# An expert-overflow loop moved ahead of the last expert pair, and the last down projection, its sum and the final norm taken by column halves

## Chip, cores and metric

The kernel runs on one core of a Trainium2 chip. The metric is the device time of one launch in microseconds (us). The kernel before has a median of 1254.08 us over 3 runs (1251.48 to 1255.8).

## The reference

Two transformer blocks run in a row on 256 tokens of width 1024. The change touches only the end of the second: a mixture of 32 experts of which every token uses two, a residual, and a last RMS norm.

```python
def hier_moe(h, w_rg, b_rg, w_re, b_re, w_gate, w_up, w_down):
    ...
    top_val, top_idx = lax.top_k(in_grp, MOE_TOP_K)
    gate = grp_p[:, None] * jax.nn.softmax(top_val, axis=-1)
    ...
    def run_block(args):
        xb, e = args
        hid = jax.nn.silu(xb @ w_gate[e]) * (xb @ w_up[e])
        return hid @ w_down[e]
    ...
    out = jnp.zeros((T + 1, D), jnp.float32).at[slot_tok].add(
        ys.astype(jnp.float32) * slot_gate[:, None])[:T]

def second_block(x, c, ada_w, ada_b, norm_mix_g, norm_ffn_g, final_g,
    ...
        h = rmsnorm_2(x, norm_ffn_g[i]) * (1 + sc2) + sh2
        x = x + g2 * hier_moe(h, moe_w_rg[i], moe_b_rg[i], moe_w_re[i], moe_b_re[i],
                              moe_w_gate[i], moe_w_up[i], moe_w_down[i])
    return rmsnorm_2(x, final_g)
```

## The kernel before

All weights are f32 and are read once. Every expert has 6 MB: gate, up and down matrices of 2 MB, each in two blocks of 1 MB. Experts go in 16 pairs (`for i in range(NP)`, L1752), and a pair needs 12 tiles of 1 MB; `moe_w` holds tiles 0 to 191 in that order, so the last pair is tiles 180 to 191. Tile q goes into slot q mod 21 of a ring made of five pools (names in the trace: ew, nw, raw, wr, hl). `preload(n)` (L1115) issues loads on SP until n tiles are issued; `weights(b)` of pair i calls it with 12 i + 2 b + 21. SP gives its loads the semaphores DMAHW0 to DMAHW7 in turn and waits for the old one before it issues a new one.

Each expert has 64 token slots in these pairs, whose token rows (`xg`) are gathered ahead. `expert` (L1614) does for a pair the blocks b = 0 to 3: b = 0 and 1 gate, b = 2 and 3 up, each of 8 matmuls, four per expert; the two experts fill the two halves of the 128 output rows. Then the SiLU (ACT) and the product `hid` (DVE). `down` (L1636) first calls `back(0)` and `back(1)`, which hold the previous pair's way back to the tokens (`combine2`, sums in four PSUM banks `acc`) and this pair's `way_back` (transposes of the one-hot matrix, L1603), then does blocks b = 4 and 5 of the down matrix into two banks `py` of the tag "w", which has two buffers.

In the last pair (`final`), `spread(0)` (L1713) puts the row g2 on all partitions between gate and up; `back` calls `gather_up` (L1723) for both token halves: R = acc * g2 + X, eight DVE operations, and after that `way_back` copies its result (L1611). At `back(5)` four matmuls with a zero (`zo`, L1773) open the `acc` banks again. After `down`, DVE multiplies both halves of `py` by g2 into `y` (L1659).

An expert with over 64 tokens needs more blocks of 64. Their number is in `nblk`, computed on the chip. After the last pair each engine loads it (L1786), and a loop `tc.For_i(0, n_more, 1)` (L1787) does one block per turn, loading 6 tiles by itself. Then the tail: four f32 matmuls (`combine`, L1671) bring `y` back to the tokens, DVE adds them to R, ACT squares and sums (L67), POOL raises to -1/2 (L253), `spread(1)` puts the norm's gain on all partitions, DVE scales (L79), and SP issues four output DMAs (L1835).

The engines' order is the program's order; nothing is reordered between engines except by waits.

Of the kernel before, what the change touches and what calls it, by code (L numbers as in the profile page):

```python
# [18 lines left out]
D = 1024  # L19
# [21 lines left out]
def kernel(ctx, tc, A, out, stop=None):  # L41
# [1556 lines left out]

    def way_back(oh_g, n, exact=False, into=None):
# [35 lines left out]

    def down(hid, weights, n_e, y, before=lambda j: None, scaled=False, gates_of=None):  # L1636
        n = 64 * n_e
# [6 lines left out]
        before(1)  # L1644
        py = [pbank("w"), pbank("w")]
        for b in range(4, 6):
            ws = weights(b)
            before(b)
            for kk in range(2):
                k = 2 * (b - 4) + kk  # L1650
                for c in range(2):
                    for e in range(n_e):
                        T.matmul(py[c][64 * e:64 * e + 64, :], hT[:, k, 64 * e:64 * e + 64],  # L1653
                                 ws[e][:, kk * 1024 + c * 512:kk * 1024 + (c + 1) * 512],
                                 start=k == 0, stop=k == 3)
        if scaled:
            for c in range(2):
                sl = slice(512 * c, 512 * c + 512)
                tt(y[:n, sl], py[c][:n], end[0][:n, sl], MUL)  # L1659
        else:  # L1660
            gc = gates_of()
            for c in range(2):
                sl = slice(512 * c, 512 * c + 512)
                act(yh[:, sl], py[c], AF.Copy, scale=gc)
                stt(yl[:, sl], py[c], gc, yh[:, sl].bitcast(F32), MUL, SUB)

# [5 lines left out]

    def combine2(h, og_, first, last):

        for c in range(2):
            sl = slice(512 * c, 512 * c + 512)
# [23 lines left out]

    zo = moe.tile([1, 2], BF16, name="zo")
    G.memset(zo[:, 0:1], 0.0)
    G.memset(zo[:, 1:2], 1.0)
    end = []

    def start_ends():
# [3 lines left out]
        G.dma_start(rows_[0:1, D:2 * D], A["final_g"])  # L1710
        end.extend([rows_[:, 0:D], rows_[:, D:2 * D], R, ring.tile([128, 2048], F32, name="raw", tag="raw")[:, 0:D]])

# [27 lines left out]
    def start():  # L1740
# [9 lines left out]
        V.tensor_copy(nblk, upto[0:1, 31:32])  # L1750

    for i in range(NP):  # L1752
# [5 lines left out]
        final = i == NP - 1  # L1758

        def back(j, i=i, prev=prev, final=final):  # L1760
# [6 lines left out]
            if j == 1:  # L1767
                backs[i] = way_back(onehots[i], 128, not final)
# [9 lines left out]
        hid = expert(weights, 2, (lambda: spread(0)) if final else None, None if i else start, 128 * (i % 2))  # L1778
        down(hid, weights, 2, end[3] if final else None, back, scaled=final, gates_of=lambda i=i: backs[i][1])
        prev = backs[i]  # L1780


    bt = rtile("bt", 1, pool=moe)
    V.memset(bt, 0.0)
    spare = nexts.tile([128, 2048], F32, name="nw", tag="nw")
    n_more = nc.values_load(nblk[0:1, 0:1], min_val=0, max_val=7)  # L1786
    with tc.For_i(0, n_more, 1):  # L1787
        oe = spare[:, D + 256:D + 288]
        ts(oe, upto, bt, None, ALU.is_gt)
        stt(oe, before, bt, oe, ALU.is_le, MUL)  # L1790
        tmp = moe.tile([128, 32], F32, name="more", tag="more")
        sel = moe.tile([128, 8], F32, name="sel")

        def pick(j, src):
            tt(tmp, src, oe, MUL)
            red(sel[:, j:j + 1], tmp, ADD)
        for h in range(2):
            pick(h, rank[:, h, :])
            pick(2 + h, gate[:, h, :])
        pick(4, before)  # L1800
        pick(5, iota64[:, 0:32])
        tt(sel[:, 6:7], bt, sel[:, 4:5], SUB)
        ts(sel[:, 6:7], sel[:, 6:7], 1.0, 64.0, ADD, MUL)
        ts(sel[0:1, 5:6], sel[0:1, 5:6], FAR, None, ADD)
        eid = moe.tile([1, 1], I32, name="eid")
        V.tensor_copy(eid, sel[0:1, 5:6])
        e_reg = nc.values_load(eid[0:1, 0:1], engines=(mybir.EngineType.SP,), min_val=0, max_val=NEXP - 1)
        oh_r = spare[:, D + 288:D + 544].rearrange("p (h t) -> p h t", h=2)
        oh_g = moe.tile([128, 2, 128], F32, name="oh", tag="oh_g", bufs=1)
        for h in range(2):  # L1810
            tt(sel[:, h:h + 1], sel[:, h:h + 1], sel[:, 6:7], SUB)
            for t_, sc in ((oh_r, rstd[h][:, 0:1]), (oh_g, sel[:, 2 + h:3 + h])):
                ts(t_[:, h, 0:64], iota64, sel[:, h:h + 1], sc, EQ, MUL)
        gather(oh_r, 64)
        og_ = way_back(oh_g, 64, into=spare[:, D:D + 256].rearrange("p (h t) -> p h t", h=2))

        def weights(b):
            t_ = wring.tile([128, 2048], F32, name="wr", tag="wr")
            SP.dma_start(t_, A["moe"][bass.ds(e_reg, 1), b].rearrange("a p n -> p (a n)"))
            return [t_]  # L1820
        hid = expert(weights, 1)
        y2 = spare[:, 0:D]
        down(hid, weights, 1, y2, scaled=True)
        for h in range(2):
            combine(h, og_, y2, False, False, 64)
        ts(bt, bt, 1.0, None, ADD)
    last = {}
    R, frow = end[2], end[1]

    def finish(h):  # L1830
        for c in range(2):
            sl = slice(512 * c, 512 * c + 512)
            o = R[:, h, sl]
            stt(o, R[:, h, sl], last[h], frow[:, sl], MUL, MUL)
            SP.dma_start(out[0, h * 128:(h + 1) * 128, sl], o)  # L1835

    for h in range(2):
        ss = stats.tile([128, 2], F32, name="fs", tag=f"fs{h}", bufs=1)
        for c in range(2):
            sl = slice(512 * c, 512 * c + 512)  # L1840
            combine(h, prev, end[3], False, True, cs=(c,))
            tt(R[:, h, sl], R[:, h, sl], acc[h, c], ADD)
            act(hid, R[:, h, sl], AF.Square, scale=D ** -0.5, accum_out=ss[:, c:c + 1])
        ts(ss[:, 0:1], ss[:, 0:1], EPS, ss[:, 1:2], ADD, ADD, e=G)
# [3 lines left out]
    for h in range(2):  # L1848
        finish(h)

# [174 lines left out]
```

## Time and profile before

| | us |
|---|---|
| median of 3 runs (lowest, highest) | 1254.08 (1251.48, 1255.8) |
| the profiled execution's own time | 1258.29 |
| its span in the trace | 1256.5 |
| PE, DVE, ACT busy in the span | 1191.1, 655.1, 481.4 |

A page of the profile shows one execution. Its span starts with the first and ends with the last record. Rows of the timeline give start, duration, engine, line, operation, tiles and count; equal neighbours are merged into one row (x32), and brackets tell how long the engine stood idle before and what ended that. An f32 matmul of the program leaves two records. Weight loads have rows of their own (PEld). An engine name with a q (SPq, ACTq) is that engine's sequencer: register loads, branches and waits. No row of the trace comes from lines 1788 to 1826, the loop's body.

### The profile page before, as it was taken

The numbers are of one execution on the slowest core, as the hardware profiler recorded it, in microseconds if no ns is written. First come the engines' busy times: TensorE is split into PE (matmuls) and PEld (weight loads), VectorE is DVE, ScalarE is ACT, GpSimd is POOL, SyncE is SP. The second block draws the span as 40 slices with busy tenths as digits, with TensorE's granted clock in tenths as the row PEclk, the third lists the DMA queues.
The fourth block names the chain that finished last, engine by engine and source line by source line (L and its number), as shares of the span: only waits on it lengthen the run. The fifth ranks groups of instructions, "written<-read, shape, count | busy, mean of one in ns | idle before, by whom it ended". The sixth has DMA issues, their size and how long they took to land. (4 is left out here: it accounts for less than half of the span.)

```text
span 1256.5 us, 15660 instructions
## 1 busy us (share of the span) xinstructions
PE 1191.1 (95%) x6064; PEld 816.7 (65%) x6067; DVE 655.1 (52%) x1112; ACT 481.4 (38%) x800; POOL 76.0 (6%) x105
## 2 busy tenths in 40 slices
PE   7999999999889999999998979999999999898996
PEld 5888888888777788888887947444444444343432
DVE  6767777677767687765464985422112221111114
ACT  7546544446775474444364523311101111010111
POOL 1101000001030000000003240000000000000000
PEclk9999999999999999999998989999999999999998
DMA  9644787774533189765543768699999999999992
GB/s 333 234 171 184 262 288 264 282 301 145 188 142 113 46 329 374 282 239 196 201 162 146 262 210 326 260 421 420 419 420 420 419 420 420 420 420 421 420 419 97
DMA packets 59947, 361.14 MB, mean 287 GB/s; under 512 B 7200, under 2 KB 10432, under 8 KB 21600
## 3 DMA queue, kind: packets, MB, share of 16 engines
q1 hardware_dynamic: 58752, 357.21, 73.2%
q0 software_dynamic: 976, 2.92, 0.7%
q8 instruction: 48, 0.79, 0.2%
q14 instruction: 27, 0.22, 0.1%
q10 hardware_dynamic: 144, 0.00, 0.0%
HBM read 358.15 MB, written 1.96 MB: 287 GB/s over the span
## 5 line engine op out<-in xcount | busy, mean ns | idle before, releaser
L111 PE MATMUL mm<-hl,xTh 128*128 128x512 f32 (+3 forms) x1376 | 422.1, 386 | 11.7 <-ACT hl L66 6.2
L70 DVE TENSOR_TENSOR hl<-raw,hl 128x1024 fp32r<-128x1024 f32 (+3 forms) x240 | 283.6, 1212 | 88.5 <-ACT hl L66 84.8
L111 PEld LDWEIGHTS mm<-hl,xTh 128*128 128x128 f32 x1376 | 257.0, 191 | 61.8 <-ACT hl L66 6.6
L66 ACT ACTIVATE hl<-raw 128x1024 fp32r<-128x1024 f32 (+3 forms) x240 | 240.7, 1033 | 137.3 <-PE mm L111 108.6
L111 PE MATMUL mm<-hl,xTl 128*128 128x512 f32 (+3 forms) x688 | 266.1, 387 | 2.5 <-DVE xTl L70 2.5
L111 PEld LDWEIGHTS mm<-hl,xTl 128*128 128x128 f32 x688 | 131.4, 191 | 26.0 <-DVE xTl L70 3.2
L70 DVE TENSOR_TENSOR hid<-gu,hid 128x512 f32<-128x512 f32 x16 | 11.1, 692 | 194.6 <-PE gu L1624 194.6
L111 PE MATMUL mm<-hl,aTh 128*128 128x512 f32 x352 | 109.0, 390 | 0.0
L1624 PE MATMUL gu<-hl,xg 128*64 128x512 f32 x392 | 100.9, 594 | 5.9 <-DMA hl<-in_moe_dram 5.9
L1624 PEld LDWEIGHTS gu<-hl,xg 128*64 128x64 f32 x392 | 35.0, 137 | 61.9 <-issue 50.2
L111 PEld LDWEIGHTS mm<-hl,aTh 128*128 128x128 f32 x352 | 66.1, 188 | 13.6
L79 DVE SCALAR_TENSOR_TENSOR yhl<-w,gc,yhl 128x512 fp32r<-128x512 f32 x30 | 22.4, 751 | 97.5 <-ACT yhl L66 95.7
L111 PE MATMUL mm<-hl,aTl 128*128 128x512 f32 x176 | 68.9, 391 | 0.0
L1624 PE MATMUL gu<-wr,xg 128*64 128x512 f32 x216 | 62.3, 595 | 5.8 <-DMA wr<-in_moe_dram 5.8
L80 DVE SCALAR_TENSOR_TENSOR ada<-ada,crow 128x1024 f32<-128x1024 f32 x48 | 58.4, 1220 | 8.0 <-DMA ada<-in_ada_dram 8.0
L66 ACT ACTIVATE yhl<-w,gc 128x512 fp32r<-128x512 f32 x30 | 20.5, 687 | 106.3 <-PE w L1653 106.3
L1653 PE MATMUL w<-hl,hid 128*64 128x512 f32 x184 | 48.9, 605 | 2.8 <-DVE ogT L1611 2.8
L66 ACT ACTIVATE xg<-w,modc,moe_g 128x256 f32<-128x256 f32 x32 | 18.1, 565 | 85.4 <-PE w L1594 85.4
L66 ACT ACTIVATE hid<-gu 128x512 f32<-128x512 f32 x16 | 9.6, 597 | 102.0 <-PE gu L1624 102.0
L1624 PE MATMUL gu<-raw,xg 128*64 128x512 f32 x152 | 44.7, 594 | 1.1 <-DMA raw<-in_moe_dram 1.1
L1624 PEld LDWEIGHTS gu<-wr,xg 128*64 128x64 f32 x216 | 20.4, 137 | 38.3 <-issue 25.9
L1624 PE MATMUL gu<-ew,xg 128*64 128x512 f32 x152 | 43.7, 594 | 0.4 <-DMA ew<-in_moe_dram 0.4
(459 smaller groups left out, 1503.9 us busy)
## 6 DMA issues: line engine op xcount, KB each, us to landing
raw<-in_dense_dram SPq DMA_DIRECT2D x108, 1024.0 KB, 5.2
hl<-in_moe_dram SPq DMA_DIRECT2D x72, 1024.0 KB, 19.8
wr<-in_moe_dram SPq DMA_DIRECT2D x45, 1024.0 KB, 19.9
ew<-in_moe_dram SPq DMA_DIRECT2D x29, 1024.0 KB, 19.9
raw<-in_moe_dram SPq DMA_DIRECT2D x27, 1024.0 KB, 19.9
ada<-in_ada_dram SPq DMA_DIRECT2D x48, 512.0 KB, 7.5
nw<-in_moe_dram SPq DMA_DIRECT2D x18, 1024.0 KB, 19.9
raw<-in_dense_dram SPq DMA_DIRECT2D x8, 512.0 KB, 7.1
```

The source lines that it names most:

```text
L66: return S.activation(o, i, f, bias=bias, scale=scale)
L70: return (e or V).tensor_tensor(o, a, b, op=op)
L79: return V.scalar_tensor_tensor(o, a, s, b, op0=op0, op1=op1)
L80: return V.scalar_tensor_tensor(o, a, s, b, op0=op0, op1=op1, accum_out=accum_out)
L111: T.matmul(o, lhsT, rhs, start=start, stop=stop_)
L1624: T.matmul(o[64 * e:64 * e + 64, :], xg[:, k, s0 + 64 * e:s0 + 64 * e + 64], ws[e][:, kk * 512:(kk + 1) * 512], start=k == 0, stop=k == 7)
L1653: T.matmul(py[c][64 * e:64 * e + 64, :], hT[:, k, 64 * e:64 * e + 64], ws[e][:, kk * 1024 + c * 512:kk * 1024 + (c + 1) * 512], start=k == ...
```

## The change

The loop is put in front of the last pair (`more_blocks`, called when `final`). Before it only 188 tiles are issued (`12 * (NP - 1) + AT_LOOP`, `AT_LOOP = 8`); tiles 188 to 191, the last pair's down matrices, are issued behind it. The last two tiles come in four DMAs by column halves. In the last pair both rows (`spread_ends`) are put on all partitions between gate and up; block b = 5 does column half 0 for both experts, then half 1, and half 0 is scaled, split into a high and a low part (yh, yl) while PE does half 1. The `zo` matmuls are gone: the sums of the last pair go into fresh `acc` banks, half 0 by four matmuls on the split parts (`combine2`), half 1 by two f32 matmuls (`combine`). The norm's gain is multiplied to token half 1 ahead of the norm's factor, so that ACT finishes half 1 and DVE half 0, with outputs issued from SP and ACT.

```diff
@@ preload
-            pieces = 2 if q == 6 * NEXP - 1 else 1
-            for c in range(pieces):
-                sl = slice(2048 // pieces * c, 2048 // pieces * (c + 1))
-                SP.dma_start(t_[:, sl], A["moe"][2 * pair + r % 2, r // 2, :, sl])
+            if q < 6 * NEXP - 2:
+                SP.dma_start(t_, A["moe"][2 * pair + r % 2, r // 2])
             moe_w.append(t_)
+            if q == 6 * NEXP - 1:
+                for c in range(2):
+                    for e in range(2):
+                        o, i = (w_.rearrange("p (k c n) -> p k c n", k=2, c=2)[:, :, c, :]
+                                for w_ in (moe_w[q - 1 + e], A["moe"][2 * pair + e, 5]))
+                        SP.dma_start(o, i)
@@ way_back
-        if exact:
+        if into is None:
             og_ = moe.tile([128, 2, 128], F32R, name="ogT", tag="ogT", bufs=1)
...
@@ down
+        def out(c):
...
+            if final:
+                stt(y[:, sl], py[c], gc, end[0][:, sl], MUL, MUL)
...
         for b in range(4, 6):
             ws = weights(b)
             before(b)
+            if final and b == 5:
+                for kk in range(2):
+                    for e in range(2):
+                        part(b, kk, 0, e)
+                out(0)
+                act(yh[:, 0:512], y[:, 0:512], AF.Copy)
+                tt(yl[:, 0:512], y[:, 0:512], yh[:, 0:512].bitcast(F32), SUB)
+                for kk, e in ((0, 0), (1, 0), (0, 1), (1, 1)):
+                    part(b, kk, 1, e)
+                out(1)
+                return
...
-        if scaled:
-            for c in range(2):
-                sl = slice(512 * c, 512 * c + 512)
-                tt(y[:n, sl], py[c][:n], end[0][:n, sl], MUL)
...
@@ the loop over the pairs
+    def more_blocks():
+
+        bt = rtile("bt", 1, pool=moe)
+        V.memset(bt, 0.0)
+        spare = end[3]
+        n_more = nc.values_load(nblk[0:1, 0:1], min_val=0, max_val=7)
+        with tc.For_i(0, n_more, 1):
...
+    def spread_ends():
+        spread(0)
+        spread(1, on_dve=(0, 1))
+
     for i in range(NP):
-        def weights(b, i=i):
+        final = i == NP - 1
+
+        def weights(b, i=i, final=final):
             q = 12 * i + 2 * b
-            preload(q + SLOTS)
+            preload(q + SLOTS if final else min(q + SLOTS, 12 * (NP - 1) + AT_LOOP))
             return moe_w[q:q + 2]
...
-            if final and j == 5:
-                for a in acc.values():
-                    T.matmul(a, zo[:, 0:1].to_broadcast([1, 128]), zo[:, 1:2].to_broadcast([1, 512]), start=True, stop=False)
+        if final:
+            more_blocks()
         if i:
             pair_slots(i)
...
-    bt = rtile("bt", 1, pool=moe)
-    V.memset(bt, 0.0)
-    spare = nexts.tile([128, 2048], F32, name="nw", tag="nw")
-    n_more = nc.values_load(nblk[0:1, 0:1], min_val=0, max_val=7)
-    with tc.For_i(0, n_more, 1):
...
+    for h in range(2):
+        combine2(h, og_, True, True, cs=(0,))
+    for h in range(2):
+        combine(h, og32, y, True, True, cs=(1,))
+    for c in range(2):
+        sl = slice(512 * c, 512 * c + 512)
         for h in range(2):
+            tt(R[:, h, sl], R[:, h, sl], acc[h, c], ADD)
+            act(hid, R[:, h, sl], AF.Square, scale=D ** -0.5, accum_out=ss[h][:, c:c + 1])
     for h in range(2):
-        ss = stats.tile([128, 2], F32, name="fs", tag=f"fs{h}", bufs=1)
...
+        ts(ss[h][:, 0:1], ss[h][:, 0:1], EPS, ss[h][:, 1:2], ADD, ADD, e=G)
         last[h] = stats.tile([128, 1], F32, name="fr", tag=f"fr{h}", bufs=1)
-        power(last[h], ss[:, 0:1], 1)
-    spread(1, on_dve=(0,))
-    for h in range(2):
-        finish(h)
+        power(last[h], ss[h][:, 0:1], 1)
+    for c in range(2):
+        sl = slice(512 * c, 512 * c + 512)
+        tt(fin[:, sl], R[:, 1, sl], frow[:, sl], MUL)
+    for c in range(2):
+        sl = slice(512 * c, 512 * c + 512)
+        stt(R[:, 0, sl], R[:, 0, sl], last[0], frow[:, sl], MUL, MUL)
+        SP.dma_start(out[0, 0:128, sl], R[:, 0, sl])
+        act(fin[:, sl], fin[:, sl], AF.Copy, scale=last[1])
+        S.dma_start(out[0, 128:256, sl], fin[:, sl])
```

Two places show what the build makes of it, with the semaphores that each instruction waits for. DMAHW0 to 7 count landed loads. The first place is PE at the start of the last pair: before, its matmuls follow the previous pair's down block, and the first one that reads a tile waits for that tile's load.

```order
L1653 MATMUL w<-wr,hid 64x512 x6
L1624 MATMUL gu<-wr,xg 64x512 [waits DMAHW0_49]
L1624 MATMUL gu<-hl,xg 64x512 [waits DMAHW1_49]
L1624 MATMUL gu<-wr,xg 64x512
L1624 MATMUL gu<-hl,xg 64x512
```

Now the loop's end stands in front of them; the way for zero turns passes there too.

```order
L1776 REGISTER_ALU
L1776 COMPARE_AND_BRANCH
L1776 UNCONDITIONAL_BRANCH [waits DMASW5_49,DMASW4_49,DMASW6_49,DMASW3_49,DMASW7_49,DMASW2_49,DMAHW0_49,DMASW1_49,DMAHW1_49,DMASW0_49,DMAHW2_49,SP_sequencer_49,DMAHW3_49,DVE_sequencer_49,DMAHW4_49,PE_sequencer_49,DMAHW5_49,Activation_s
L1627 MATMUL gu<-wr,xg 64x512
L1627 MATMUL gu<-hl,xg 64x512
L1627 MATMUL gu<-wr,xg 64x512
```

The waits for single tiles moved from the matmuls into one branch that waits for every load semaphore (the printed row breaks off; 6 and 7 follow in it) and for every engine.

The second place is SP, the queue of the loads. Before, the last pair's last loads stand ahead of the loop:

```order
L1138 DMA hl<-in_moe_dram 128x2048 [waits DMAHW0_49,PE_49]
L1138 DMA ew<-in_moe_dram 128x2048 [waits DMAHW1_49,PE_49]
L1138 DMA ew<-in_moe_dram 128x2048 [waits DMAHW2_49,PE_49]
L1138 DMA ew<-in_moe_dram 128x1024 [waits DMAHW3_49,PE_49]
L1138 DMA ew<-in_moe_dram 128x1024 [waits DMAHW4_49]
L1786 TENSOR_LOAD nblk [waits DVE_49]
```

Now:

```order
L1776 COMPARE_AND_BRANCH
L1776 UNCONDITIONAL_BRANCH [waits DMASW5_49,DMASW4_49,DMASW6_49,DMASW3_49,DMASW7_49,DMASW2_49,DMAHW0_49,DMASW1_49,DMAHW1_49,DMASW0_49,DMAHW2_49,SP_sequencer_49,DMAHW3_49,DVE_sequencer_49,DMAHW4_49,PE_sequencer_49,DMAHW5_49,Activation_se
L1136 DMA hl<-in_moe_dram 128x2048
L1136 DMA ew<-in_moe_dram 128x2048
L1143 DMA ew<-in_moe_dram 128x2x512 x4
L1873 DMA out_dram<-raw 128x512 [waits DVE_49]
```

Six loads (4 MB) moved behind the branch.

## Rows read from the trace of the kernel before

**Rows 1.** Page, the span in 40 slices: GB/s that the DMA engines moved.

```profile
GB/s 333 234 171 184 262 288 264 282 301 145 188 142 113 46 329 374 282 239 196 201 162 146 262 210 326 260 421 420 419 420 420 419 420 420 420 420 421 420 419 97
```

**Rows 2.** Page, DMA issues: tiles, queue, count, KB each, median us to landing.

```profile
raw<-in_dense_dram SPq DMA_DIRECT2D x108, 1024.0 KB, 5.2
hl<-in_moe_dram SPq DMA_DIRECT2D x72, 1024.0 KB, 19.8
```

**Rows 3.** Timeline, the last pair's gate and up, ahead of it pair 14's down.

```profile
1198.37 7.34 PE L1653 MATMUL w<-wr,hid 128*64 128x512 f32 x32
...
1212.00 3.65 PE L1624 MATMUL gu<-hl,xg 128*64 128x512 f32 x14 [1.33 <-DMA hl<-in_moe_dram]
...
1215.58 1.98 PE L1717 MATMUL w<-raw,ones 1*128 1x512 f32 x4
...
1217.49 8.14 PE L1624 MATMUL gu<-hl,xg 128*64 128x512 f32 x32
...
1221.99 0.20 PEld L1624 LDWEIGHTS gu<-hl,xg 128*64 128x64 f32 x4 [0.87 <-DMA hl<-in_moe_dram]
...
1225.57 0.50 PE L1677 MATMUL acc<-yhl,ogT 128*128 128x512 f32 x1
```

**Rows 4.** Line 1787 (the loop): ns min/median/max, first and last start in us.

```profile
L1787 SPq EVENT_SEMAPHORE  x19: 17/28/11103, 1215.9 to 1242.1; - x19
L1787 ACTq EVENT_SEMAPHORE  x13: 17/38/11103, 1227.9 to 1242.2; - x13
L1787 PEldq EVENT_SEMAPHORE  x13: 51/51/51, 1241.2 to 1243.0; - x13
...
L1787 PEldq COMPARE_BRANCH  x3: 101/187/325, 1238.2 to 1243.1; - x3
```

**Rows 5.** Waits of SP's queue from 1214 us on: total, times, longest.

```profile
SPq L1787 <- SPq L1787: 13.6, 3, 8.6
```

**Rows 6.** Timeline, PE after its longest idle time in mid-kernel.

```profile
740.44 9.57 PE L1261 MATMUL mm<-u,taps 128*32 128x256 f32 x128 [4.54 <-POOL taps L70]
```

**Rows 7.** Stretches: us, length, PE, PEld, DVE, ACT, POOL busy, granted clock, DMA, GB/s.

```profile
740.00:741.00 1.00, 0.56 (x8) 0.33 (x12) 1.00 (x1) 0.00 (x0) 0.39 (x1) 0.50 0.99 410
...
745.00:746.00 1.00, 1.00 (x20) 0.49 (x16) 1.00 (x4) 0.42 (x1) 0.83 (x1) 0.77 0.61 246
...
1234.00:1235.00 1.00, 1.00 (x4) 0.24 (x2) 0.00 (x0) 0.00 (x0) 0.00 (x0) 0.50 0.00 0
```

**Rows 8.** Timeline: pair 14's way back on DVE, then the last pair's down.

```profile
1198.47 0.42 DVE L83 TENSOR_REDUCE gc<-w 128x1 f32<-128x256 f32 x1 [1.95 <-PE w L1603]
...
1198.82 0.41 DVE L74 TENSOR_SCALAR ogT<-w 128x256 fp32r<-128x256 f32 x1
...
1232.18 0.64 PE L1653 MATMUL w<-hl,hid 128*64 128x512 f32 x1 [2.82 <-DVE ogT L1611]
...
1236.18 1.41 PE L1773 MATMUL acc<-zo 1*128 1x512 bf16 x4
...
1237.52 3.65 PE L1653 MATMUL w<-ew,hid 128*64 128x512 f32 x16
```

**Rows 9.** Timeline of the tail.

```profile
1240.39 1.52 DVE L70 TENSOR_TENSOR raw<-w,raw 128x512 f32<-128x512 f32 x2 [8.27 <-PE w L1653]
...
1243.34 5.40 PE L1671 MATMUL acc<-raw,ogT 128*128 128x512 f32 x8 [2.16 <-issue]
...
1248.70 0.63 ACT L67 ACTIVATE hid<-raw 128x512 f32<-128x512 f32 x1 [0.46 <-DVE raw L70]
...
1249.56 0.63 ACT L67 ACTIVATE hid<-raw 128x512 f32<-128x512 f32 x1
...
1250.38 0.30 POOL L75 TENSOR_SCALAR fs<-fs 128x1 f32<-128x1 f32 x1 [1.07 <-ACT hid L67]
1250.65 2.74 DVE L79 SCALAR_TENSOR_TENSOR raw<-raw,fr 128x512 f32<-128x512 f32 x4
...
1250.77 1.05 POOL L253 TENSOR_TENSOR fr<-fs,mhalf 128x1 f32<-128x1 f32 x1
```

More of the change, by code (lines that the diff above doesn't have):

```diff
@@ L1597, in gather2, with way_back @@
                 gather_out(2 * g + i, tp[:, i, :], 256)
-    def way_back(oh_g, n, exact=False, into=None):
+    def way_back(oh_g, n, into=None):
         tp = pbank("w")
@@ L1634, in expert, with down @@
         return hid
-    def down(hid, weights, n_e, y, before=lambda j: None, scaled=False, gates_of=None):
+    def down(hid, weights, n_e, y, before=lambda j: None, gates_of=None, final=False):
         n = 64 * n_e
@@ L1671, in combine, with combine2 @@
             T.matmul(acc[h, c], og_[:n, h, :], y[:n, c * 512:(c + 1) * 512], start=first, stop=last)
-    def combine2(h, og_, first, last):
-        for c in range(2):
+    def combine2(h, og_, first, last, cs=(0, 1)):
+        for c in cs:
             sl = slice(512 * c, 512 * c + 512)
@@ L1710, in start_ends @@
         G.dma_start(rows_[0:1, D:2 * D], A["final_g"])
[L1711 removed]
+        end.extend([rows_[:, 0:D], rows_[:, D:2 * D], R, ring.tile([128, 2048], F32, name="raw", tag="raw")])
     def spread(j, on_dve=()):
@@ L1750, in start, with pick, weights @@
         V.tensor_copy(nblk, upto[0:1, 31:32])
+    def more_blocks():
[4 more added lines that the diff above has]
+        with tc.For_i(0, n_more, 1):
+            oe = spare[:, D + 256:D + 288]
+            ts(oe, upto, bt, None, ALU.is_gt)
+            stt(oe, before, bt, oe, ALU.is_le, MUL)
+            tmp = moe.tile([128, 32], F32, name="more", tag="more")
+            sel = moe.tile([128, 8], F32, name="sel")
+            def pick(j, src):
+                tt(tmp, src, oe, MUL)
+                red(sel[:, j:j + 1], tmp, ADD)
+            for h in range(2):
+                pick(h, rank[:, h, :])
+                pick(2 + h, gate[:, h, :])
+            pick(4, before)
+            pick(5, iota64[:, 0:32])
+            tt(sel[:, 6:7], bt, sel[:, 4:5], SUB)
+            ts(sel[:, 6:7], sel[:, 6:7], 1.0, 64.0, ADD, MUL)
+            ts(sel[0:1, 5:6], sel[0:1, 5:6], FAR, None, ADD)
+            eid = moe.tile([1, 1], I32, name="eid")
+            V.tensor_copy(eid, sel[0:1, 5:6])
+            e_reg = nc.values_load(eid[0:1, 0:1], engines=(mybir.EngineType.SP,), min_val=0, max_val=NEXP - 1)
+            oh_r = spare[:, D + 288:D + 544].rearrange("p (h t) -> p h t", h=2)
+            oh_g = moe.tile([128, 2, 128], F32, name="oh", tag="oh_g", bufs=1)
+            for h in range(2):
+                tt(sel[:, h:h + 1], sel[:, h:h + 1], sel[:, 6:7], SUB)
+                for t_, sc in ((oh_r, rstd[h][:, 0:1]), (oh_g, sel[:, 2 + h:3 + h])):
+                    ts(t_[:, h, 0:64], iota64, sel[:, h:h + 1], sc, EQ, MUL)
+            gather(oh_r, 64)
+            og_ = way_back(oh_g, 64, into=spare[:, D:D + 256].rearrange("p (h t) -> p h t", h=2))
+            def weights(b):
+                t_ = nexts.tile([128, 2048], F32, name="nw", tag="nw")
+                SP.dma_start(t_, A["moe"][bass.ds(e_reg, 1), b].rearrange("a p n -> p (a n)"))
+                return [t_]
+            hid = expert(weights, 1)
+            down(hid, weights, 1, spare[:, 0:D])
+            for h in range(2):
+                combine(h, og_, spare[:, 0:D], False, False, 64)
+            ts(bt, bt, 1.0, None, ADD)
@@ L1777 @@
             ones2[0] = two_pairs(i + 1)
-        hid = expert(weights, 2, (lambda: spread(0)) if final else None, None if i else start, 128 * (i % 2))
-        down(hid, weights, 2, end[3] if final else None, back, scaled=final, gates_of=lambda i=i: backs[i][1])
+        hid = expert(weights, 2, spread_ends if final else None, None if i else start, 128 * (i % 2))
+        down(hid, weights, 2, end[3] if final else None, back, gates_of=lambda i=i: backs[i][1], final=final)
         prev = backs[i]
-    bt = rtile("bt", 1, pool=moe)
@@ L1784 @@
-    V.memset(bt, 0.0)
-    spare = nexts.tile([128, 2048], F32, name="nw", tag="nw")
-    n_more = nc.values_load(nblk[0:1, 0:1], min_val=0, max_val=7)
-    with tc.For_i(0, n_more, 1):
[L1788 to L1796, printed above, removed]
-        for h in range(2):
[L1798 to L1809, printed above, removed]
-        for h in range(2):
[L1811 to L1826, printed above, removed]
@@ L1847 @@
-    spread(1, on_dve=(0,))
-    for h in range(2):
-        finish(h)
+    last, R, frow = {}, end[2], end[1]
+    og_, y = prev[0], end[3]
+    og32 = og_.bitcast(F32)
+    fin = nexts.tile([128, 2048], F32, name="nw", tag="nw")[:, 0:D]
+    ss = [stats.tile([128, 2], F32, name="fs", tag=f"fs{h}", bufs=1) for h in range(2)]
+    for h in range(2):
+        combine2(h, og_, True, True, cs=(0,))
+    for h in range(2):
+        combine(h, og32, y, True, True, cs=(1,))
+    for c in range(2):
+        sl = slice(512 * c, 512 * c + 512)
+        for h in range(2):
+            tt(R[:, h, sl], R[:, h, sl], acc[h, c], ADD)
+            act(hid, R[:, h, sl], AF.Square, scale=D ** -0.5, accum_out=ss[h][:, c:c + 1])
```

51 lines of the change are left out of this document (19 added, 32 removed).

## The prediction

> **What bounds the kernel now.** I read the page's slices first. From slice 27 on the loads run at 419 to 421 GB/s [rows 1]: the expert stage goes at the pace of the weight stream, and PE waits for tiles. Then the DMA issues: a 1 MB tile lands 19.8 us after its issue, against 5.2 us where loads are sparse [rows 2]; at 420 GB/s (2.5 us a tile) that is eight tiles in flight, as many as there are load semaphores. The timeline of the last pair shows the pace. The first matmul on tile 183 starts at 1212.00 and the first on tile 187 at 1221.99, both released by a load [rows 3], so tiles land 9.99 / 4 = 2.50 us apart, and tile 187, the last of the gate and up matrices, is there at 1222.0. PE has done three of the four blocks by then; the sums of the way back follow at 1225.57 [rows 3]. From there to the end of the span (1256.5) the kernel is a tail of 30.9 us, of which the stream covers only the start.
>
> The rows of line 1787 matter most. The loop makes no turn on these inputs (no row from its body), yet SP stands in it for 13.6 us [rows 5] on semaphores that, by the build, are those of the loads, and then SP and ACT both sit in one wait of 11.103 us to the end of it, at 1242.2 [rows 4]. That wait thus begins at about 1231.1 in both. An engine that passes the empty loop waits there for all issued loads, then for the slowest engine (here DVE, done with y at 1241.91 [rows 9]). At the kernel's end this costs little, since everything has landed.
>
> **The drain in front of the last pair (the loss).** Now the same wait stands ahead of pair 15's first matmul, on PE too, and it covers tiles 180 to 187, which PE used to take one by one. Nothing makes the stream faster up to tile 187: the same bytes, slots and semaphores. So PE, which ends pair 14's down at 1198.37 + 7.34 = 1205.7 [rows 3], stands until 1222.0. From the last landing to PE's first matmul I take 0.5 us. The lower end is 0.15: two waits of 0.051 and the shortest branch is about 0.2, less what overlaps [rows 4]. The upper end is 1.4, from DVE's end at 1241.91 to PE's matmul at 1243.34 [rows 9]. But there PE had only just come into the loop; here it will have stood at the last wait for long, as ACT and SP did, so I stay near the lower end. Restart: 1222.5.
>
> *Cold clock.* PE will have stood for some 16 us. After its 4.54 us of idleness PE restarted at 740.44 [rows 6] with a granted clock of 0.50, the 1.2 GHz level, and was back at 1.00 within the stretch 745 to 746, whose mean is 0.77, so at about 745.5 [rows 7]. That is 5.0 us at half rate, 2.5 us lost. Ends: 0 and 2.6; a longer idle time gives no reason for a smaller price, so 2.5. [...] The trace shows the 2.5 us, and they lie on the path here.
>
> *Gate and up on their own.* Two blocks in a row take between 7.2 (twice the 3.58 from 1212.00 to 1215.58, where a load still released the first matmul [rows 3]) and 6.9 (the 7.34 of as many matmuls, those of pair 14's down, less the end of the last one, which a next matmul overlaps by about one record's 0.43 [rows 3]). Nothing releases them here, so 6.9, and 13.8 for four; the other end is 0.6 more. One spread takes 1215.58 to 1217.49 = 1.91 [rows 3]; the change puts the second one beside it, which adds the copies out of its two banks (ACT, DVE) beside PE: 3.8 for both. So the way back begins at 1222.5 + 2.5 + 13.8 + 3.8 = 1242.6 instead of 1225.57: **+17.0 us**.
>
> *The four late tiles.* SP issues them at about 1222.5. First landing 5.2 us later [rows 2], three more tiles at 2.5: all there by 1235.3. Block 4 needs its tiles at 1242.6 + 2.7 (the old distance to the first down matmul) = 1245.3. Ten us of cover, even if the strided halves came at half the rate (5 us more). Costed at nothing; were they later, each us would be a us.
>
> **The down block.** Still one stall: `gather_up`'s eight DVE operations keep `way_back` waiting, and PE with it for 2.82 us [rows 8]. `way_back` now reduces and compares instead of copying: the next operation starts 0.35 us after the reduce [rows 8], so **+0.35**. The `zo` matmuls go: 1236.18 to 1237.52 = **-1.34** [rows 8]. Block 5's half 1 takes one expert's two matmuls ahead of the other's, so their overlap is lost once: between 0 and 2 x 0.86, and I take one matmul of two records, **+0.86**. The dip to 0.50 in this block [rows 7] stays, since the stall does. Together -0.1.
>
> **The tail.** Before: from PE's last down matmul (1241.17 = 1237.52 + 3.65 [rows 8]) to 1256.5, 15.3 us. It held DVE's two products (1.52), the loop, four f32 matmuls at half clock (5.40), and the last sums [rows 9]. Now, from the last down matmul on: half 0 is already split, since its product, copy and difference take some 2.4 us beside 2.6 us of half 1. DVE's scaling of half 1: 0.15 + 0.75. Then DVE is the chain: four sums of 0.69 (half of 1.37 for two products [rows 9]), PE's matmuls beside them, end 3.7. ACT's squares start at 1.7 after the first sum and follow each other by 0.86 (1248.70 to 1249.56 [rows 9]): end 5.1. POOL for token half 1: 0.1 + 0.30 + 0.1 + 1.05 [rows 9], 6.7. ACT's two scalings 0.6 each: 7.9. Last output: 3.1 us as before (1253.39 to 1256.5 [rows 9]). 11.0 us, so **-4.3**; the PE matmuls could cost up to 1.7 more in a new dip, and POOL up to 0.5 less.
>
> Sum: 17.0 - 0.1 - 4.3 = **+12.6 us**. Against the profiled execution: span 1269.1, time 1270.9. That execution (1258.29) lies 4.2 us over the median of the runs, so the median goes from 1254.08 to **1266.7**. No change means within 0.3%, 3.8 us, about what a measurement can tell.
>
> **Rivals.**
>
> 1. *The loop holds only SP, PE goes on (faster).* Then gate and up keep the stream's pace, the way back begins at 1225.6, and only the late tiles move: issued at 1222.0, all there at 1234.8, needed from 1232.5 on by a block that takes them in turn. Price 0 to 1, gain 4.4: 1249.7 to 1250.7. It decides at one point: whether PE's first gate matmul of the last pair comes before 1222.0. For it: zero turns are run. Against: PE's branch waits for every load in the build, and ACT and SP, which have no use for the tiles, waited in rows 4. [...] Chance 5%.
>
> 2. *The late tiles are late.* After the drain the queue starts empty, and halves of 2 KB rows are slower than half rate. It decides when they land after 1245.3; for block 5, which needs the halves from 1252 on, that would take over 29 us for 4 MB. A loss of 0 to 5: up to 1271.7. Nothing in the rows speaks for it. Chance 7%.
>
> 3. *The restart is dearer.* The engines fetch the code behind the loop late: 1.4 us instead of 0.5, a new dip in the tail 1.7, together +2.6: 1269.3. Chance 18%.
>
> 4. *The drain is half hidden (no change).* It would need the stream to be some 9 us ahead at that point, but the releases at 1212.00 and 1221.99 show no slack. 1254 to 1258. Chance 3%.
>
> The forecast, 67%: the drain, the cold restart and the shorter tail as summed.
>
> **How the numbers follow.** Forecast and rivals 2 and 3 are all slower: 0.67 + 0.07 + 0.18 = 0.92. Rival 1 is faster, 0.05. Rival 4 is no change, 0.03. The range leaves out rivals 1 and 4 and the far end of 2. Its lower end takes the bounds of the clock (-2.5) and of the overlap (-0.9) and a us of spread between medians: 1262.0. Its upper end is rival 3 with the same spread and the overlap's other bound (+0.9): 1271.5.
>
> **What would show it.** Right: PE has no matmul between about 1205.7 and 1222.5; all queues have a long wait on the loop's line that ends just after tile 187 lands; the first gate matmuls follow at a granted clock of 0.50 for some 5 us; the way back begins near 1242.6; the last six loads are issued after 1222 and land 10 us ahead of their use; from the last down matmul to the end it takes 11 us instead of 15.3. Wrong: a gate matmul of the last pair before tile 187's landing (rival 1), PE waiting for a load in the down block (rival 2), a gap of over 1 us between landing and restart (rival 3).

## The result and the profile after

The changed kernel takes 1270.88 us (median of 4 runs, 1270.27 to 1271.57) against 1254.94 us (1251.48 to 1256.08): ratio 1.0132, 95% interval 1.011 to 1.0153, so 13.8 to 19.2 us slower. Its profiled execution took 1270.27 us with a span of 1268.6.

To compare spans I count from the start of pair 14's down block, called P here: 1198.37 before [rows 3], 1197.28 after. What lies ahead of P is the same program. From P on the last part has three stages, a block's end taken as its last record's start and length:

| kernel | P to way back | to end of last down matmul | to end | sum |
|---|---|---|---|---|
| before, the execution of the prediction | 27.20 | 15.60 | 15.33 | 58.13 |
| changed | 43.67 | 14.99 | 12.66 | 71.32 |

The timeline of the changed kernel (start, us, engine, line, operation, idle time before it and what ended it):

```profile
1197.28 7.32 PE L1652 MATMUL w<-wr,hid 128*64 128x512 f32 x32
...
1206.11 0.06 DVE L1773 MEMSET bt<- 128x1 f32 x1
...
1221.26 1.11 PE L1627 MATMUL gu<-wr,xg 128*64 128x512 f32 x1 [16.66 <-DMA hl<-in_moe_dram]
...
1221.94 2.71 SPq L1143 DMA_DIRECT2D ew<-in_moe_dram  x4
...
1225.39 0.59 PE L1627 MATMUL gu<-wr,xg 128*64 128x512 f32 x1
...
1230.21 3.79 PE L1735 MATMUL w<-raw,ones 1*128 1x512 f32 x8
...
1240.95 0.49 PE L1698 MATMUL acc<-yhl,ogT 128*128 128x512 f32 x1
...
1247.99 0.61 PE L1652 MATMUL w<-hl,hid 128*64 128x512 f32 x1 [3.25 <-DVE ogT L74]
...
1251.27 4.67 PE L1652 MATMUL w<-ew,hid 128*64 128x512 f32 x17
```

PE ends pair 14 at 1204.6 and has nothing until 1221.26: 16.66 us, ended by a load. Three of the four blocks of gate and up, which PE had done before by the time tile 187 landed [rows 3], now start behind that landing. In the trace tile 187's load has its last update at 1220.78, 0.48 us ahead of PE's first matmul. The loop's line, by queue (count: ns min/median/max, first and last start in us):

```profile
L1776 SPq EVENT_SEMAPHORE  x19: 17/28/28, 1202.4 to 1220.9; - x19
L1776 PEldq EVENT_SEMAPHORE  x13: 51/51/51, 1204.6 to 1220.9; - x13
L1776 ACTq EVENT_SEMAPHORE  x13: 17/38/38, 1205.4 to 1221.2; - x13
```

Every engine comes to it at another time and all leave at 1220.9 to 1221.2; before, that was so at the end of the kernel [rows 4]. One row for each stretch shows the clock (last three columns: granted clock, DMA, GB/s):

```profile
1207.00:1208.00 1.00, 0.00 (x0) 0.00 (x0) 0.00 (x0) 0.00 (x0) 0.00 (x0) 1.00 1.01 410
1208.00:1209.00 1.00, 0.00 (x0) 0.00 (x0) 0.00 (x0) 0.00 (x0) 0.00 (x0) 0.57 0.99 401
...
1220.00:1221.00 1.00, 0.00 (x0) 0.00 (x0) 0.00 (x0) 0.00 (x0) 0.00 (x0) 0.50 0.00 0
...
1224.00:1225.00 1.00, 1.00 (x6) 0.34 (x4) 0.00 (x0) 0.00 (x0) 0.00 (x0) 0.50 1.00 410
1225.00:1226.00 1.00, 1.00 (x6) 0.28 (x4) 0.00 (x0) 0.00 (x0) 0.00 (x0) 0.90 1.05 426
...
1235.00:1236.00 1.00, 1.00 (x8) 0.29 (x4) 0.00 (x0) 0.00 (x0) 0.00 (x0) 1.00 0.06 23
1237.00:1238.00 1.00, 1.00 (x8) 0.42 (x6) 0.00 (x0) 0.00 (x0) 0.00 (x0) 1.00 0.00 0
```

The granted clock fell to 0.50 while PE stood (0.57 at 1208) and rose behind the restart, at about 1225 (0.90). The loads go on at 401 to 434 GB/s until 1217; then the queue runs dry, down to nothing at 1220, since SP stands in the loop too and issues its next load at 1221.08. The loads issued behind the loop are all there by about 1236, 8 us ahead of the down block (1243.66). The tail:

```profile
1256.97 2.01 DVE L70 TENSOR_TENSOR raw<-raw,acc 128x512 f32<-128x512 f32 x3
...
1259.76 1.28 DVE L70 TENSOR_TENSOR nw<-raw 128x512 f32<-128x512 f32 x2
...
1260.10 1.03 POOL L75 TENSOR_SCALAR fs<-fs 128x1 f32<-128x1 f32 x1 [68.98 <-ACT hid L67]
1260.55 0.18 ACT L67 ACTIVATION_READ_ACCUMULATOR hid<-raw 128x1 f32 x1
1261.21 0.56 POOL L253 TENSOR_TENSOR fr<-fs,mhalf 128x1 f32<-128x1 f32 x1
...
1261.88 0.85 POOL L75 TENSOR_SCALAR fs<-fs 128x1 f32<-128x1 f32 x1
...
1262.81 0.84 POOL L253 TENSOR_TENSOR fr<-fs,mhalf 128x1 f32<-128x1 f32 x1
1263.69 0.72 ACT L66 ACTIVATE nw<-nw,fr 128x512 f32<-128x512 f32 x1 [2.95 <-POOL fr L253]
1264.44 0.35 ACTq L1875 DMA_DIRECT2D out_dram<-nw  x1
1264.84 0.72 ACT L66 ACTIVATE nw<-nw,fr 128x512 f32<-128x512 f32 x1 [0.43 <-ACT nw L66]
1265.59 0.34 ACTq L1875 DMA_DIRECT2D out_dram<-nw  x1
```

POOL's small step, 0.30 us before [rows 9], takes 1.03 and 0.85 beside DVE's products. POOL does both steps of token half 0 first, so the step of half 1 begins at 1261.88, 1.15 us after ACT's squares are done (1260.73). The store that ACT issues stands between its two scalings.

### The profile page after: what moved, and what is told of

Read it like the earlier page. It is cut to its first block, busy times and chain, and to the rows that moved or that the text cites. A ratio compares the mean times of both kernels' runs of the same rounds, so it can differ in the third digit from the quotient of the medians.

```text
span 1268.6 us, 15646 instructions
## 1 busy us (share of the span) xinstructions
PE 1185.9 (93%) x6060; PEld 815.6 (64%) x6063; DVE 656.7 (52%) x1115; ACT 483.3 (38%) x802; POOL 77.0 (6%) x103
## 4 chain that ended last, share of the span: by engine, by line
PE 71%; DMA 17%; DVE 5%; ACT 4%; issue 1%; POOL 1%; POOLq 0%; ACTq 0%; SPq 0%; DVEq 0%
PE mm L111 47%; PE gu L1627 11%; DMA hl<-in_moe_dram 8%; PE w L1652 5%; DMA nw<-in_moe_dram 3%; DMA raw<-in_moe_dram 2%; DMA wr<-in_moe_dram 2%; DMA ew<-in_moe_dram 2%; ACT hl L66 1%; DVE hl L70 1%; PE w L1598 1%; PE acc L1698 1%; DMA cs<-in_xT_dram 1%; PE tp L597 1%; DVE yc L79 1%
## 5 line engine op out<-in xcount | busy, mean ns | idle before, releaser
L111 PE MATMUL mm<-hl,xTh 128*128 128x512 f32 (+3 forms) x1376 | 420.2, 385 | 12.6 <-ACT hl L66 6.4
L80 DVE SCALAR_TENSOR_TENSOR ada<-ada,crow 128x1024 f32<-128x1024 f32 x48 | 58.4, 1219 | 5.9 <-DMA ada<-in_ada_dram 5.8
```

The lines of the kernel that those rows point to most:

```text
L80: return V.scalar_tensor_tensor(o, a, s, b, op0=op0, op1=op1, accum_out=accum_out)
L111: T.matmul(o, lhsT, rhs, start=start, stop=stop_)
```

## The experiments

The theory: the loop's empty pass drains the load queue, PE stands until tile 187 has landed, and that is the loss; halves and the new norm change little. The rivals: the loss lies in the order by halves and its late strided loads; or in the loop's pass itself wherever it stands.

**The change, and its parts.**

x0_change is the changed kernel again.

> The changed kernel once more, so that the parts below are compared with it on one chip. Drain theory: 1270 to 1271.5 us, 16 us (13 to 19) over the kernel before. If the medians before the study were only unlucky draws of the kernel before, the difference comes out near the 12 us by which the two profiled spans differ (1268.6 less 1256.5).

x1_loop: the kernel before, with only the loop moved, and with it the cap on the loads (the lines below show the call alone).

```diff
+        if final:
+            more_blocks()
         if i:
             pair_slots(i)
```

> The kernel before with nothing but the loop moved in front of the last pair (and the load cap that goes with it); last down block, sums and final norm as before. Drain theory: the way back begins some 14.5 us later, counted from the start of pair 14's down (16.5 in the changed kernel, less 1.9 for the second spread, which stays in the tail); the tail loses the loop's wait at the end, 1.4 us. Together +13: 1268 us (1266 to 1270). Rival, the loss comes from the order by column halves (its strided late loads, its lost overlap): then this kernel is within 2 us of before, 1253 to 1257.

x2_tail: the changed kernel with the loop behind the last down block again.

```diff
-        if final:
-            more_blocks()
...
+    hid = more_blocks()
     last, R, frow = {}, end[2], end[1]
...
-            preload(q + SLOTS if final else min(q + SLOTS, 12 * (NP - 1) + AT_LOOP))
+            preload(q + SLOTS)
```

> The changed kernel with the loop back behind the last down block, loads uncapped, the acc banks opened by the zero matmuls as before; column halves, gates in the way back, both spreads side by side and the new final norm stay. Drain theory: no restart of PE; the second spread delays the way back by up to 0.8 us; from the last down matmul to the end 14.6 us (12.7 in the changed kernel and 2 for the loop's wait in between) instead of 15.3. So about the time of before: 1253 to 1256 us. Rival, the halves carry the loss: 1264 to 1271.

x3_noloop: the changed kernel without `more_blocks` and without the cap.

> The changed kernel without the loop at all (with these inputs it makes no turn; experts with over 64 tokens would lose their surplus), loads uncapped. Drain theory: everything but the drain stays, so 28.0 us from the start of pair 14's down to the way back (27.2 before and 0.8 for the second spread) and 27.6 from there to the end, 55.6 against 58.1 before: 2.5 us faster than before, 1252.4 us (1250.5 to 1254), 18 us faster than the change. Rival, the loss is in the halves or in the late strided loads: over 1262.

Measured, with the stages as above:

| run | median us | ratio to before, interval | P to way back | to last down | to end | sum |
|---|---|---|---|---|---|---|
| x0_change | 1270.2 | 1.0129, 1.011 to 1.0147 | 43.76 | 15.00 | 12.63 | 71.39 |
| x1_loop | 1268.44 | 1.0111, 1.0092 to 1.0129 | 42.15 | 15.68 | 11.43 | 69.26 |
| x2_tail | 1258.36 | 1.0031, 1.0018 to 1.0045 | 29.63 | 14.45 | 14.54 | 58.62 |
| x3_noloop | 1254.14 | 0.9997, 0.9984 to 1.001 | 29.61 | 16.03 | 13.13 | 58.77 |

The loop alone carries the loss: x1_loop came out at 1268.4 for an expected 1268, and PE stands in it as in the changed kernel:

```profile
1221.47 1.12 PE L1624 MATMUL gu<-wr,xg 128*64 128x512 f32 x1 [16.69 <-DMA hl<-in_moe_dram]
```

The halves with the loop at its old place cost 0.3% and not 1.3%. But x2_tail is slower than I expected, and x3_noloop by a little; the stages say where. They are those of one execution each, and x3_noloop's took 1257.52 us, 3.4 over its median, with two stretches at 0.50, so its sum is not that of its median run. Once the loop has left the end, the **old** tail takes 11.43 us (x1_loop), the new one 12.6 to 13.1. In x1_loop the sums follow the down block at once and at full clock:

```profile
1251.62 3.65 PE L1653 MATMUL w<-ew,hid 128*64 128x512 f32 x16
1255.24 3.70 PE L1674 MATMUL acc<-raw,ogT 128*128 128x512 f32 x8
```

Before, the same eight records took 5.40 us behind a wait of 2.16 [rows 9]. So the old tail lost its 3.9 us to the loop: 2.2 to the wait and 1.7 to the clock that had fallen behind it. And with no drain ahead, both spreads side by side cost 2.4 us up to the way back (29.6 for 27.2), not 0.8: the clock falls right behind them in both, while PE works and the loads run at full pace (x3_noloop):

```profile
1217.00:1218.00 1.00, 1.00 (x4) 0.20 (x4) 0.83 (x2) 0.00 (x0) 0.00 (x0) 1.00 1.03 418
1219.00:1220.00 1.00, 1.00 (x4) 0.24 (x2) 0.00 (x0) 0.00 (x0) 0.00 (x0) 0.50 1.03 426
...
1222.00:1223.00 1.00, 1.00 (x8) 0.38 (x6) 0.00 (x0) 0.00 (x0) 0.00 (x0) 1.00 1.06 424
```

**How many tiles ahead of the loop.** x4_at2 and x5_at12 differ from the changed kernel by one number.

```diff
-AT_LOOP = 8
+AT_LOOP = 2
```

> The changed kernel with AT_LOOP = 2: only tiles up to 181 are issued ahead of the loop, so the drain ends when 181 lands, some 2 us after PE's own end of pair 14's down, and no long idle time of PE stands in front of gate and up; but then SP issues the last ten tiles into an empty queue. Drain theory: the wait at the loop shrinks from 16.7 to about 2 us, and a new one appears at the tiles behind it, since they begin 7 us late: way back 3 to 6.5 us later than before instead of 16.5, total 1257 to 1261 us. Rival, it is the loop's own entry (code, branches, the restart of all engines) that costs, not the loads it waits for: no better than 1267.

> The changed kernel with AT_LOOP = 12: all tiles are issued ahead of the loop, so it waits for tile 191 too, some 9 to 10 us longer, and no load is left for afterwards. Drain theory: PE restarts 9 to 10 us later, the rest as in the changed kernel: 1279 to 1281 us. Rival, part of the loss comes from the last six loads that are issued behind the loop: then this kernel gives that part back and stays below 1277.

x5_at12: 1280.95 us, 1.0198 (1.0181 to 1.0215), as expected; PE stands for 27.36 us until the last tile of all has landed:

```profile
1231.81 1.12 PE L1627 MATMUL gu<-wr,xg 128*64 128x512 f32 x1 [27.36 <-DMA ew<-in_moe_dram]
```

Nothing is gained by having no late loads. In its profile PE restarts 10.7 us later behind P than in the changed kernel; more time at 0.50 in gate and up and in the down block costs another 2.3. That the late loads of the changed kernel cost nothing shows in its own trace: no wait of PE behind the restart is ended by a load. x4_at2: 1262.92 us, 1.005 (1.0031 to 1.0068), above the expected 1257 to 1261, yet 7 to 8 us below the change:

```profile
1208.28 0.64 PE L1627 MATMUL gu<-wr,xg 128*64 128x512 f32 x1 [2.44 <-DVEq L1776]
...
1216.52 5.33 PE L1627 MATMUL gu<-hl,xg 128*64 128x512 f32 x14 [2.41 <-DMA hl<-in_moe_dram]
...
1225.49 8.78 PE L1627 MATMUL gu<-hl,xg 128*64 128x512 f32 x32
```

The pass now costs PE 2.44 us, and tiles come late behind it (2.41). The 5.33 and the 8.78 each hold a stretch at 0.50 that I hadn't counted. The loss goes with the tiles that the loop waits for.

**The loop where nothing waits.** In the last pair, between the way back and the down block, all loads have long been issued and PE waits anyway [rows 8]. x6_mid has the changed kernel's tail, with the second spread just ahead of the loop, x7_mid_old_tail that of before; in both the final sums start fresh banks, so x7 needs no zero matmuls. The edit in x7:

```diff
                 backs[i] = way_back(onehots[i], 128, not final)
+                if final:
+                    more_blocks()
+                    gather_up(0)
+                    gather_up(1)
```

> The changed kernel with the loop between the last pair's way back and its down block, loads uncapped, the sums of the way back read out behind the loop, the second spread just ahead of it. Drain theory: at that point everything has been issued for long, PE has nothing to do until the last tiles land, and DVE has 5.3 us of sums that can now run beside the down block; the loop then costs under 1 us, and the tail is that of the changed kernel. 1251 to 1254 us, at or below the kernel before, 16 to 19 us below the change. Rival, a loop ahead of a block costs its 16 us wherever it stands: over 1262.

> The kernel before with the loop between the last pair's way back and its down block; the acc banks start afresh in the final sums, so the zero matmuls go; products, sums and norm at the end as before. From the parts measured so far (the kernel with the loop alone moved had 11.4 us from its last down matmul to the end, the changed one 12.6, the kernel before 15.3): 54 us from the start of pair 14's down instead of 58.1, 1250 to 1252 us, the fastest of all. If the new order by halves is worth what was forecast (4.3 us in the tail), the run before this one is faster instead.

x6_mid: 1254.64 us, 0.9984 (0.9973 to 0.9994); stages 27.17, 16.26, 12.64. x7_mid_old_tail: 1253.35 us, 0.998 (0.9969 to 0.9991); stages 27.18, 15.98, 11.36. Both lie 0.6 and 1.4 us above what was expected, but they are 0.2% **faster than before** and 16 to 18 us faster than the change; the old tail is again 1.3 us shorter. In x7:

```profile
1230.85 0.64 PE L1654 MATMUL w<-hl,hid 128*64 128x512 f32 x1 [4.40 <-DMA ew<-in_moe_dram]
...
1235.61 4.03 PE L1654 MATMUL w<-ew,hid 128*64 128x512 f32 x17
...
1239.57 3.70 PE L1675 MATMUL acc<-raw,ogT 128*128 128x512 f32 x8
```

PE now waits 4.40 us, until the last tile has landed, where before it waited 2.82 for DVE [rows 8]; `gather_up` runs beside the down block instead of ahead of it. So the pass isn't dear by itself. The gain over before is 2 to 2.5 us, near what can be measured.

**The cold restart.** x8_busy, x11_busy17: the changed kernel with 34 and 17 idle matmuls ahead of the loop. x9_mid_busy, x12_mid_busy4: x7 with 9 and 4.

```diff
+                    keep_busy(4)
                     more_blocks()
```

> The changed kernel with 34 matmuls of 128x512 (idle work on constant data into the two free gate/up banks, some 15.7 us of PE) ahead of the loop, so that PE isn't idle while the loads drain. Theory of a cold clock: the 3.9 us at 0.50 behind the restart go, 1.9 us come back: 1268.5 us, with the drain itself (end of the loop's wait, last landing) unmoved. Rival, the restart is slow for another reason (code fetched late, a queue): 1270 to 1271, and the first matmuls still take 1.06 us. If PE comes late to the loop the gain is smaller by what it is late.

> The fastest kernel so far (loop between the last way back and the down block, old tail) with 9 such idle matmuls, 3.9 us of PE, ahead of the loop, where PE waited 4.4 us for the last tiles. If the dip to 0.50 in its down block (3.4 us, 1.7 lost) comes from this wait: 1.5 us less than that kernel, 1251.5 to 1252.5, 0.3 to 0.4% below before. Rival, the dip comes anyway, or in the tail instead: no change, 1253 to 1254.

> The changed kernel with 17 idle matmuls (two records of 0.43 us each, 14.7 us of PE) ahead of the loop, so that PE is done about a microsecond before the last landing. Theory of a cold clock: the stretch at 0.50 behind the restart goes, 1.9 us come back, 1268.5 to 1269 us. Rival, the restart is slow for another reason: 1270 to 1271, first matmuls still 1.06 us.

> The kernel with the loop between the last way back and the down block and with the old tail, with 4 idle matmuls (3.5 us of PE) ahead of the loop, within the 4.4 us that PE waited there. The run with 9 of them had no stretch at 0.50 in the down block, but PE came 3.5 us late. So 1.5 us less than without: 1251.5 to 1252.5, some 0.35% below the kernel before. Rival, PE's late entry into the loop costs 2.2 us as it did there, whatever the loads do: 1254 or more.

In x8 and x9 I took one record for one matmul; each of these f32 matmuls left two (17 of them are the 34 of the x11_busy17 row below). PE was held for 29.45 and 7.89 us and came last to the loop: 1285.76 us, 1.0236 (1.0214 to 1.0259), and 1256.73 us, 1.0012 (0.9998 to 1.0025). They show a price, though: 2.15 and 2.16 us from PE's last matmul ahead of the loop to the first behind it. x11_busy17 fails too: 1272.3 us, 1.013 (1.011 to 1.015), no gain.

```profile
1203.30 14.86 PE L1819 MATMUL gu<-X,ident 128*128 128x512 f32 x34
...
1220.31 1.11 PE L1627 MATMUL gu<-wr,xg 128*64 128x512 f32 x1 [2.15 <-DMA hl<-in_moe_dram]
```

```profile
1219.00:1220.00 1.00, 0.00 (x0) 0.00 (x0) 0.00 (x1) 0.00 (x0) 0.00 (x0) 1.00 0.06 16
...
1221.00:1222.00 1.00, 1.00 (x4) 0.24 (x2) 0.00 (x0) 0.00 (x0) 0.00 (x0) 0.50 0.43 115
```

The granted clock held at 1.00 while PE was kept busy and fell all the same after the 2.15 us, to 0.50 at 1221 (in x8_busy it held at 1.00 through a gap as long); later it fell once more behind the spreads (0.50 at 1234), which it doesn't do in the changed kernel. The restart's 2 us could not be bought back this way. x12_mid_busy4: 1252.74 us, 0.9979 (0.9965 to 0.9993), 0.2 above what was expected. There the down block has no stretch at 0.50 (15.48 us instead of 15.98), but PE, busy until 1228.98, starts 1.2 us later than in x7, again 2.15 us behind its last idle matmul. The two runs are the same within their intervals; both beat the kernel before.

**The tail's POOL steps.** x10_stt: the changed kernel with the last step of the norm as before.

```diff
-    for c in range(2):
-        tt(fin[:, sl], R[:, 1, sl], frow[:, sl], MUL)
...
+            stt(R[:, h, sl], R[:, h, sl], last[h], frow[:, sl], MUL, MUL)
+            SP.dma_start(out[0, h * 128:(h + 1) * 128, sl], R[:, h, sl])
```

> The changed kernel with the last step of the norm as before: four products on DVE, each behind the power of its token half, all stores from SP; no product of token half 1 in advance, no scalings on ACT. If the missing part of the forecast's tail (12.7 us instead of 11.0) is POOL, whose four small operations ran beside DVE's products in advance (1.03 and 0.85 us for a step that takes 0.30 alone), and ACT, whose two scalings have a store's issue between them: 1.2 to 1.8 us come back, 1268.7 us. Rival, the tail is bound by the sums and squares ahead of that: within 0.5 us of the changed kernel.

1269.78 us, 1.0111 (1.0093 to 1.013); last stage 11.48 instead of 12.66, the low end of what was expected. By the median alone it is 0.4 us below x0_change, which the runs can't tell from nothing; the gain is read from the stages. With no DVE operation beside it POOL's first step is back to 0.30; the second runs beside a product of DVE and isn't:

```profile
1260.88 0.30 POOL L75 TENSOR_SCALAR fs<-fs 128x1 f32<-128x1 f32 x1 [69.06 <-ACT hid L67]
...
1261.94 0.85 POOL L75 TENSOR_SCALAR fs<-fs 128x1 f32<-128x1 f32 x1
```

So the step takes 0.55 to 0.73 us longer beside a product of DVE here (0.85 in this run and 1.03 in the changed kernel, for 0.30 without). No run shows why.

**The kernel before, three more profiles.** b_again, b3 and b4 are the kernel before, unchanged.

> The kernel before once more, for a second profile: the profiled execution on which the prediction rests was 4.2 us over the median. If that excess lay ahead of the expert stage, this execution differs ahead of pair 14's down, and the 58.1 us from there to the end stay. If it lay in the last 58 us, then in stretches at a granted clock of 0.50 that come in some executions and not in others: then these 58.1 us change by 1.7 for each such stretch.

> A third profile of the kernel before. The two so far have 58.1 us from the start of pair 14's down to the end, with the same two stretches at a granted clock of 0.50. If the spread of its times (1251 to 1258) lies there, an execution near 1252 has 54 to 55 us and lacks one or both stretches; if it lies ahead, the 58.1 stay and pair 14 starts earlier.

> A fourth profile of the kernel before, as the third: 58.1 us and an earlier or later pair 14, or another length of the last part.

| execution | time us | P | P to way back | to last down | to end | sum |
|---|---|---|---|---|---|---|
| the prediction's | 1258.29 | 1198.37 | 27.20 | 15.60 | 15.33 | 58.13 |
| b_again | 1256.71 | 1196.92 | 27.17 | 15.61 | 15.30 | 58.08 |
| b4 | 1257.51 | 1197.70 | 27.18 | 15.61 | 15.31 | 58.10 |
| b3 | 1253.51 | 1197.13 | 27.18 | 13.96 | 13.53 | 54.67 |

b3 keeps a granted clock of 1.00 where the other three fall to 0.50 [rows 7]:

```profile
1234.00:1235.00 1.00, 1.00 (x6) 0.29 (x5) 0.00 (x0) 0.00 (x0) 0.00 (x0) 1.00 0.00 0
```

```profile
1234.62 3.65 PE L1653 MATMUL w<-ew,hid 128*64 128x512 f32 x16
1240.37 3.70 PE L1671 MATMUL acc<-raw,ogT 128*128 128x512 f32 x8 [2.09 <-issue]
```

So the same kernel has 3.4 us more or less in its last part, 1.65 in the down block and 1.8 in the tail, as the clock falls behind PE's two waits or not.

Each run on record lists its mean granted clock, and that says the same. Of the 78 runs of the kernel before beside these experiments, the 32 at 0.990 or more took 1251.3 to 1255.6 us (median 1253.3), the 28 at 0.988 or less 1255.1 to 1260.8 (median 1257.6). The prediction's execution, at 0.987, is of the second kind. The nine runs of the changed kernel all lie at 0.980 to 0.983 and took 1269.1 to 1271.6. The mean doesn't show in which stage the clock fell.

## Why the prediction was right and wrong

The side and the mechanism were right: slower, by the drain. The size was short: 12.6 forecast, 15.9 between medians. 1270.88 lies inside the stated range, near its upper end, and that is partly luck: this end was set by rival 3, a late restart and a new dip in the tail, and neither came. (Added up again from their own terms the ends are 1266.7 - 2.5 - 0.9 - 1.0 = 1262.3 and 1269.3 + 1.0 + 0.9 = 1271.2.) By its steps:

- **Drain.** Forecast: PE has no matmul from 1205.7 to 1222.5, 16.8 us, and restarts 24.1 behind P. Measured: 16.66 and 23.98. Rivals 1 and 4 fell with it. The dearer restart of rival 3 did not come: from the landing at 1220.78 to PE's first matmul at 1221.26 it is 0.48 us, 0.5 forecast, and no run shows the late fetch of code that it supposes; nor did its dip in the tail, where the sums run at full clock.
- **Cold clock.** Forecast 2.5, measured 2.0: from 1221.26 to 1225.39 PE made five steps, which take 2.15 at full clock (0.43 each; the four whole ones at 0.50 took 0.85 to 0.90). The 1.2 GHz that the prediction sets beside 0.50 is an estimate, at one column a clock: in the kernel before, with 0.50 granted from 757 to 759, bf16 matmuls of 512 columns (L128) start at 756.16, 756.59 and so on to 758.72, six steps of 0.43 us, 1.2 columns a ns. The price is 2.0 us of a span of 1268.6. But what the clock gives and takes in the last part (3.4 us from one execution of before to the next) is as large as what a measurement can tell here.
- **Gate and up, spreads.** Restart to way back: 20.1 forecast, 19.7 measured. With the clock's share right to 0.5 us, the terms held. From P the way back comes 16.5 us later, forecast 17.0.
- **Late tiles.** Costed at nothing, and so it was: 8 us of cover were left, and PE waited for none of them. Rival 2 fell: from 1223 to 1233 the late loads moved 256 to 426 GB/s, over half of 420.
- **Down block.** Forecast -0.1, measured -0.6; its stall grew from 2.82 to 3.25 for a forecast 0.35.
- **The tail: failed.** "11.0 us, so -4.3": it took 12.66, so -2.7. The squares were done 4.8 us behind the last down matmul, 5.1 forecast. From there to the factor of token half 1 the sum has 1.6, and it took 2.9: it left out that POOL does half 0's two steps first, and it put the small step at 0.30, which took 1.03 and 0.85 beside DVE's products. ACT's two scalings, put at 0.6 each with nothing between, took 1.9 (0.72 each, and 0.43 with the store's issue between them). And the old order without the loop was not costed at all: x1_loop shows that it has 11.43, of which the new order gives 1.2 back.
- **From the profile to the median: failed, and the larger error.** The prediction says that "that execution (1258.29) lies 4.2 us over the median of the runs", and takes the 4.2 off the changed kernel too. Against the changed kernel's own profile the forecast was close, 1270.9 us for 1270.27, but by errors that cancel: 1.6 short in the tail, 0.5 too much in the way back and in the down block each, and a P that came 1.1 us earlier. The 4.2 us were not common to both kernels. By the four profiles 3.4 of them are the two stretches at 0.50, which three executions of the kernel before have and one lacks; the rest lies ahead of P, which that execution reached 0.7 to 1.5 us later than the other three. From the 58.13 the change costs 13.2 us, from the 54.67 of b3 it costs 16.65; the 15.9 between medians lies between. The two profiles of the changed kernel and that of x10_stt all have the cold restart and one more stretch in the down block, and the runs of the changed kernel lie closer together in clock and in time. Its median is 0.6 us above its profile, not 4.2 below.

What stays open: why the clock falls behind the two spreads in x2_tail to x5_at12 and x11_busy17 (and within them in x8_busy) and not in the changed kernel, and why the same wait of PE costs it in some executions and not in others. No run was made on that.

## What to carry to other kernels

In these kernels a hardware loop is a point at which every engine waits for every load already issued, even if it makes no turn: in the changed kernel the five queues left it at 1220.9 to 1221.2, behind the landing at 1220.78, and with four more tiles issued ahead of it (x5_at12) PE stood 27.36 us instead of 16.66. Look for such a point by the semaphore rows of the loop's line, and put it where the queue is empty and the engines wait anyway (1253.35 us in x7_mid_old_tail), not ahead of a block that the loads feed one tile at a time (1270.88). Before an excess of the profiled execution over the median is carried over to the changed kernel, find the stage that it lies in. One more profile of the unchanged kernel may not do, since two of the three taken here were like the first; the mean granted clock of each run showed two kinds. When a part is moved out of a tail, time the old tail without it first: its gain may have nothing to do with the new order that is put in its place.

## What the runs showed of the hardware

- The pass of an empty loop costs PE 2.1 to 2.2 us from its last matmul to its next when PE comes late (2.09 in b3, 2.16 before [rows 9], 2.15 in x8_busy, x11_busy17 and x12_mid_busy4), but PE starts only 0.48 us behind the last landing when it has stood there for long, as in the changed kernel. On PE the three compare-and-branch rows took 101 to 325 ns [rows 4]; no row here shows a branch by itself. The passage as a whole is over six times the longest of them.
- In x3_noloop the granted clock fell to 0.50 (at 1219) while PE was booked busy in all rows around, right behind the eight matmul records of the two spreads. Behind the same eight it stayed at 1.00 in the changed kernel (at 1235). No run shows why.
